# Seven products for 8 of 11 pairs of weight tiles instead of 5, made three and then four together, with weight sums made in DRAM

## The chip, the cores and the metric

One NeuronCore of a Trainium2 chip runs the whole program. The metric is the device time of one execution in microseconds, the median of several runs.

## The reference, cut to what matters

Two decoder layers on 512 positions of width 1024, all in float32. Each layer has a token mixer (multi-scale pooling in layer 0, differential attention in layer 1) and then the same gated feed-forward network, whose last product the change touches:

```python
def conv_ffn(h, w_up, conv_w, conv_b, w_down):      # h (1, 512, 1024), w_up (1024, 5632), w_down (2816, 1024)
    u = h @ w_up
    u = causal_dwconv(u, conv_w, conv_b)            # 3 taps along the positions
    a, g = jnp.split(u, 2, axis=-1)
    return (jax.nn.silu(g) * a) @ w_down

for i in range(DEPTH):
    ...
    x = x + conv_ffn(rmsnorm(x, norm_g[i, 1]), w_up[i], conv_w[i], conv_b[i], w_down[i])
return rmsnorm(x, final_norm)
```

## The kernel before, in words

**Precision.** A float32 product is three TensorE matmuls on rounded parts: each operand is split into `hi` (a cast on ScalarE, ACT) and `lo = x - hi` (a subtraction on VectorE, DVE), line 157 and 158, and `mm3` (lines 176 to 178) adds hi·hi, hi·lo and lo·hi in PSUM.

**The feed-forward network, `ffn`.** The up projection goes through 22 steps `f`. Each makes two tiles of 128 channels by 512 positions, 8 x 3 matmuls of 512 columns for the gate and as many for the value, and `gate` (convolution, silu, product) turns them into one activation tile. Weights come as chunks of 128 x 1024 (`chunk`): SyncE (SP) issues the load into one of 3 `raw` buffers, ACT and DVE split it into one each of 5 `hi` and 5 `lo` buffers.

**The down projection.** 22 activation tiles are 11 pairs `kk`. The output is x, four row tiles of 128 positions by two column halves `dh` of 512. For the last 6 pairs it is done the plain way (`pair`, weights from `pair_weights`): 2 column halves x 4 row tiles x 2 tiles x 3 matmuls. For the first 5 (`SEVEN`) a pair is a 2 x 2 block product, positions halved (`left`, `right`) and columns halved, done as in Strassen's method with seven block products. The activations' seven forms (differences of quarter blocks) are made by `forms` on DVE and split. The weights' forms are a block, a difference of two (on DVE, line 465) or a sum of two. A sum is made by DMA: SP loads one block into SBUF, and a GpSimd (POOL) DMA adds the other to it in place (line 461). `PLACES` says to which quarters of the output a product is added or subtracted (`put`, line 490); products 6 and 7 go to one quarter only and share PSUM banks with plain pairs. `GROUPS` packs the pairs' weights as two chunks for two pairs each and a half chunk for one.

**Order.** TensorE executes in the order of the program text. In the down projection that is the list of steps in `PASSES`, one string per column half: `p0` is plain pair 5, `5a` product 5 of the pairs of group a, `f2` the forms of pair 2, `e5` the additions of product 5, `k3` loads weights that are kept. The other engines' orders are fixed at compile time by a planner with its own costs, in which an instruction that comes earlier in the text goes first when both are ready. A buffer is taken from a pool when an earlier tile in it has been released. Forms of pairs 2 to 4 are made in the down projection (`LATE`), in the sixteen 512-column places of the two `H` buffers, which the up projection's input leaves free. The three plain pairs that are kept end the stage: per row tile 18 matmuls, the last addition, and `after`, which is the next stage's norm in layer 0 (`to_n2`) and the final norm and store in layer 1 (`finish`).

Of the kernel before, what the change touches and what calls it, by code (L numbers as in the profile page):

```python
# [38 lines left out]
SEVEN, LATE = 5, 2  # L39
GROUPS = (0, 2), (2, 2), (4, 1)  # L40


SIDES = {1: ((0, 0), ALU.subtract, (1, 1)), 2: ((0, 0), None, None), 3: ((0, 1), ALU.add, (1, 1)),
         4: ((1, 0), ALU.add, (0, 0)), 5: ((1, 1), None, None), 6: ((0, 0), ALU.add, (0, 1)),
         7: ((1, 0), ALU.add, (1, 1))}
PLACES = {1: ((0, 0, ALU.add), (1, 1, ALU.add)), 2: ((1, 0, ALU.add), (1, 1, ALU.subtract)),
          3: ((0, 1, ALU.add), (1, 1, ALU.add)), 4: ((0, 0, ALU.add), (1, 0, ALU.add)),
          5: ((0, 0, ALU.add), (0, 1, ALU.subtract)), 7: ((0, 0, ALU.add),)}

PASSES = ("p0 5a p1 f2 2a 7a f3 p2 f4 5b 5c e5 p3 2b 2c e2 p4 1a 1b p5 s 1c e1 7b 7c e7",  # L50
          "p0 4a 4b p1 4c e4 d 3a p2 3b 3c e3 6a 6b 6c k3 k4 k5")
# [26 lines left out]
def trunk(ctx, tc, x, norm_g, pool_w, pool_scale, kv_norm, w_kv, wq, lam, subln_g, wo,  # L78
# [10 lines left out]
    psum = ctx.enter_context(tc.tile_pool(name="psum", bufs=8, space=bass.MemoryType.PSUM))  # L89
    ctx.enter_context(tc.manual_schedule(engines={mybir.EngineType.PE}))  # L90
# [287 lines left out]
    def ffn(l, hT, cw, ws, pss, after):  # L378
# [13 lines left out]
        def gate(f, pg, pa):  # L392
            late = LATE <= f // 2 < SEVEN
# [12 lines left out]

        left, right = slice(0, HALF), slice(HALF, S)

        def forms(kk, room):


            a, b = act.pop(2 * kk), act.pop(2 * kk + 1)
            f = wide(f"f{l}_{kk}")
            less = ALU.subtract
            nc.vector.tensor_tensor(v3(f[:, :S], 2), v3(a, 2), b[:, right].unsqueeze(1).to_broadcast([P, 2, HALF]), less)
            nc.vector.tensor_tensor(f[:, S:S + HALF], a[:, left], b[:, left], less)
            nc.vector.tensor_tensor(f[:, S + HALF:], a[:, right], a[:, left], less)
            nc.vector.tensor_tensor(b[:, left], b[:, left], b[:, right], less)
            name = f"{l}_{kk}"
            both = room(f"fa{name}")  # L420
            split(a[:, left], both[:, left], both[:, right])
            form[kk, 3] = both[:, left], both[:, right]
            for src, one, two in (f[:, :S], 1, 2), (f[:, S:], 5, 6), (b, 7, 4):
                hi, lo = room(f"fh{name}_{one}"), room(f"fl{name}_{one}")
                split(src, hi, lo)
                form[kk, one] = cols((hi, lo), 0, HALF)
                form[kk, two] = cols((hi, lo), HALF, S)
# [17 lines left out]
        rooms = [v[:, i * S:(i + 1) * S] for v in halls for i in range(KD)]  # L445

        def room(name):
            return rooms.pop() if rooms else big(name)

        def block(kk, n, j, dh):  # L450

            src = w_down[l, kk * 2 * P:(kk + n) * 2 * P, dh * S:(dh + 1) * S]
            return src.rearrange("(k j p) c -> p j k c", j=2, p=P)[:, j]

        def product_weights(i, kk, n):
            name = f"d{l}_{i}_{kk}"
            first, op, other = SIDES[i]
            raw, hi, lo = chunk(block(kk, n, *first), n, S, name,
                                wide(f"rs_{name}")[:, :n * S] if op == ALU.add else None)
            if op == ALU.add:  # L460
                nc.gpsimd.dma_start(out=v3(raw, n), in_=block(kk, n, *other), accum_op=ALU.add)  # L461
            elif op:
                more = wide(f"raw2_{name}")[:, :n * S]
                nc.sync.dma_start(out=v3(more, n), in_=block(kk, n, *other))
                nc.vector.tensor_tensor(raw, raw, more, op)
            split(raw, hi, lo)
            return hi, lo

        def seven(i, kk, n, pss, first=None, last=None):

            w = product_weights(i, kk, n)
            for t in range(2):
                for k in range(n):
                    mm3(pss[t], cols(form[kk + k, i], t * P, (t + 1) * P), cols(w, k * S, (k + 1) * S),
                        kk + k == first, kk + k == last)
# [16 lines left out]
        def put_all(i):  # L492
            for half, dh, op in PLACES[i]:
                for t in range(2):
                    put(at[i][t], 2 * half + t, dh, op)

        at, kept = {}, []
        for dh in range(2):
            pss = [bank(f"pd{l}{dh}{t}") for t in range(NT)]
            at[7 - dh] = pss[2 * dh:2 * dh + 2]  # L500
            for step in PASSES[dh].split():
                if step[0] == "f":
                    forms(int(step[1:]), room)
                elif step[0] == "p":
                    kk = SEVEN + int(step[1:])
                    w = pair_weights(kk, dh)
                    for t in range(NT):
                        pair(pss[t], t, kk, w, kk == SEVEN, dh == 0 and kk == NF // 2 - 1 and t > 1)
                elif step[0] == "k":
                    kk = SEVEN + int(step[1:])  # L510
                    kept.append((kk, pair_weights(kk, dh)))
                elif step[0] == "e":
                    put_all(int(step[1:]))
                elif step[0] == "s":
                    for t in (2, 3):
                        put(pss[t], t, 0)
                elif step[0] == "d":
                    for t in range(NT):
                        after(t, 0)
                else:  # L520
                    i, (kk, n) = int(step[0]), GROUPS["abc".index(step[1])]
                    if i not in at:
                        at[i] = [bank(f"pd{l}_{i}{t}") for t in range(2)]
                    own = i < 6
                    seven(i, kk, n, at[i], 0 if own else None, SEVEN - 1 if own or i == 7 else None)
# [8 lines left out]
    def to_n2(t, dh):  # L534
        if dh == 0:
# [274 lines left out]
    def finish(t, dh):  # L810
        half_square(t, dh)
        if dh == 0:
# [55 lines left out]
```

## Time and profile before

| | us |
|---|---|
| median of 3 runs | 991.2 (990.95 to 993.31) |
| profiled execution, its own time | 991.5 |
| span of the profiled execution | 989.7 |
| PE busy | 978.0 (99%) |
| DVE busy | 641.8 (65%) |
| ACT busy | 451.0 (46%) |
| POOL busy | 113.5 (11%) |

Starting from 0, the up projection of layer 0 lies in about 40 to 280 us, its down projection to 394, attention to 640, and layer 1's up and down projections to the end. An operation is named out<-in with the program's names, buffer numbers left out: `pd<-hi_d,ah` is a matmul into a bank of the down projection from a weight chunk's high part and an activation's high part, `pu` one of the up projection, `raw_u` and `rs_d` weight buffers. Matmuls overlap, so the distance between their starts says more than the time of one.

### The profile page before, as it was taken

How to read it: one execution, taken by the hardware profiler on the slowest of the kernel's cores; microseconds unless marked ns; L12 is line 12 of the kernel's file. 1: busy time of each engine (PE TensorE's matmuls, PEld its weight loads, DVE VectorE, ACT ScalarE, POOL GpSimd, SP SyncE). 2: the span in 40 equal slices, each digit the busy share in tenths (PEclk: the TensorE clock that was granted, in tenths of full speed). 3: DMA queues.
4: the chain of work that ended last, by engine and by line, in shares of the span. 5: the costliest groups of instructions: out<-in, count | busy, mean ns of one | idle time of the engine just before them, and what ended most of it. 6: DMA issues, size and time to landing. Idle time of an engine off the chain costs nothing.

```text
span 989.7 us, 12569 instructions
## 1 busy us (share of the span) xinstructions
PE 978.0 (99%) x4810; PEld 826.9 (84%) x4810; DVE 641.8 (65%) x1000; ACT 451.0 (46%) x713; POOL 113.5 (11%) x137
## 2 busy tenths in 40 slices
PE   8999999999999999999999999999999999999997
PEld 8998888888888888788888887988888888888885
DVE  5877666665675545467867797687666656666553
ACT  5554334444462334346756763464334444452341
POOL 4500000000001111361220101000000000000211
PEclk9999999999999999999999999999999999999999
DMA  8333533323247963243213211233523233247952
GB/s 263 111 107 90 145 95 97 103 89 107 85 158 199 252 151 107 82 138 100 65 43 107 65 43 43 86 108 105 148 86 107 87 106 95 98 144 218 249 129 90
DMA packets 139783, 116.33 MB, mean 118 GB/s; under 512 B 4162, under 2 KB 112331, under 8 KB 139723
## 3 DMA queue, kind: packets, MB, share of 16 engines
q1 hardware_dynamic: 134218, 105.04, 34.0%
q0 software_dynamic: 5504, 10.49, 6.5%
q8 instruction: 38, 0.62, 0.3%
q14 instruction: 23, 0.18, 0.1%
HBM read 113.41 MB, written 2.10 MB: 117 GB/s over the span
## 4 chain that ended last, share of the span: by engine, by line
PE 96%; DVE 1%; DMA 1%; SPq 0%; issue 0%; POOL 0%; ACT 0%; DVEq 0%; POOLq 0%; ACTq 0%
PE pu L176 16%; PE pu L177 16%; PE pu L178 16%; PE pd L176 8%; PE pd L178 8%; PE pd L177 8%; PE sc L637 2%; PE po L666 2%; PE pw L178 2%; PE pj_k L178 1%; PE pj_k L176 1%; PE pj_k L177 1%; PE pj_q L177 1%; PE pj_q L176 1%; PE pj_q L178 1%; PE pw L177 1%
## 5 line engine op out<-in xcount | busy, mean ns | idle before, releaser
L158 DVE TENSOR_TENSOR lo_u<-raw_u,hi_u 128x1024 fp32r<-128x1024 f32 x84 | 103.2, 1231 | 122.7 <-ACT hi_u L157 122.5
L176 PE MATMUL pu<-n3h,hi_u 128*128 128x512 f32 (+1 forms) x384 | 142.9, 372 | 0.0
L176 PE MATMUL pu<-n1h,hi_u 128*128 128x512 f32 (+1 forms) x384 | 142.8, 372 | 0.0
L177 PE MATMUL pu<-n1l,hi_u 128*128 128x512 f32 (+1 forms) x384 | 142.6, 371 | 0.0
L177 PE MATMUL pu<-n3l,hi_u 128*128 128x512 f32 (+1 forms) x384 | 142.6, 371 | 0.0
L178 PE MATMUL pu<-n1h,lo_u 128*128 128x512 f32 (+1 forms) x384 | 142.6, 371 | 0.0
L178 PE MATMUL pu<-n3h,lo_u 128*128 128x512 f32 (+1 forms) x384 | 142.6, 371 | 0.0
L157 ACT CAST hi_u<-raw_u 128x1024 fp32r<-128x1024 f32 x84 | 88.3, 1053 | 106.9 <-PE pu L177 101.9
L461 POOL DMA_DIRECT2D rs_d<-in_w_down_dram x24 | 27.0, 1189 | 609.5 <-DMA rs_d<-in_w_down_dram 409.6
L176 PEld LDWEIGHTS pu<-n3h,hi_u 128*128 128x128 f32 x384 | 72.3, 188 | 12.6
L178 PEld LDWEIGHTS pu<-n3h,lo_u 128*128 128x128 f32 x384 | 72.3, 188 | 12.6
L177 PEld LDWEIGHTS pu<-n1l,hi_u 128*128 128x128 f32 x384 | 72.3, 188 | 12.5
L178 PEld LDWEIGHTS pu<-n1h,lo_u 128*128 128x128 f32 x384 | 72.3, 188 | 12.5
L176 PEld LDWEIGHTS pu<-n1h,hi_u 128*128 128x128 f32 x384 | 72.3, 188 | 12.4
L177 PEld LDWEIGHTS pu<-n3l,hi_u 128*128 128x128 f32 x384 | 72.3, 188 | 12.3
L176 PE MATMUL pd<-hi_d,ah 128*128 128x512 f32 x192 | 74.8, 389 | 0.0
L178 PE MATMUL pd<-hi_d,al 128*128 128x512 f32 x192 | 74.7, 389 | 0.0
L177 PE MATMUL pd<-lo_d,ah 128*128 128x512 f32 x192 | 74.7, 389 | 0.0
L157 ACT CAST hi_d<-raw_d 128x1024 fp32r<-128x1024 f32 (+1 forms) x42 | 41.7, 993 | 65.4 <-PE pd L178 48.1
L158 DVE TENSOR_TENSOR lo_d<-raw_d,hi_d 128x1024 fp32r<-128x1024 f32 (+1 forms) x42 | 47.5, 1147 | 32.7 <-ACT hi_d L157 32.7
L395 ACT ACTIVATE cv<-cv 128x512 f32<-128x512 f32 x44 | 27.8, 632 | 81.0 <-DVE cv L389 80.9
L387 ACT ACTIVATE cv<-pu,c_cb,c_cw 128x512 f32<-128x512 f32 x76 | 58.9, 776 | 0.0
(193 smaller groups left out, 1936.0 us busy)
## 6 DMA issues: line engine op xcount, KB each, us to landing
raw_u<-in_w_up_dram SPq DMA_DIRECT2D x88, 512.0 KB, 3.8
raw_d<-in_w_down_dram SPq DMA_DIRECT2D x40, 512.0 KB, 4.7
rs_d<-in_w_down_dram SPq DMA_DIRECT2D x16, 512.0 KB, 4.9
rs_d<-in_w_down_dram POOLq DMA_DIRECT2D x16, 512.0 KB, 7.1
raw_v<-in_w_kv_dram SPq DMA_DIRECT2D x8, 512.0 KB
raw_q<-in_wq_dram SPq DMA_DIRECT2D x8, 512.0 KB, 4.0
raw_k<-in_w_kv_dram SPq DMA_DIRECT2D x8, 512.0 KB
raw_o<-in_wo_dram SPq DMA_DIRECT2D x8, 512.0 KB, 3.4
```

What stands on the lines that cost most here:

```text
L157: nc.scalar.copy(hi, src)
L158: nc.vector.tensor_tensor(lo, src, hi, ALU.subtract)
L176: nc.tensor.matmul(ps, lh, rh, start=first, stop=False)
L177: nc.tensor.matmul(ps, lh, rl, start=False, stop=False)
L178: nc.tensor.matmul(ps, ll, rh, start=False, stop=last)
L387: nc.scalar.activation(y, ps, AF.Identity, bias=w[3], scale=w[2])
L395: nc.scalar.activation(y, y, AF.Silu)
L461: nc.gpsimd.dma_start(out=v3(raw, n), in_=block(kk, n, *other), accum_op=ALU.add)
L637: nc.tensor.matmul(ps[:, :m], qs[h, c][:, q], k[:, :m], start=not last, stop=bool(last))
L666: nc.tensor.matmul(po[h][:, qi * P:(qi + 1) * P], aT[:, kt * P:(kt + 1) * P], vt[kt][h // 4][:, (h % 4) * VD:(h % 4 + 1) * VD], start=kt = ...
```

## The change

Eight pairs, not five, go the way of seven products (`SEVEN` = 8), in four groups of two; three pairs stay plain. The list of steps is replaced by written loops with two passes. The first has products 5, 6 and 3 of each group in turn and then the plain pairs' right column half; the second has products 1, 4, 7 and 2 of each group in turn and then the plain pairs' left half, row tile by row tile. `forms` is cut into `forms_one` (products 5, 6, 3) and `forms_two` (1, 2, 7, 4). Forms of pairs 0 to 2 are made during the up projection, those of pairs 3 to 7 late, each call before the group or pair that it is written ahead of. A difference of weights is made on DVE from two loaded chunks. A sum of weights no longer goes through SBUF: during steps 2 to 17 of the up projection, one sum a step, POOL copies one block to a DRAM tile and adds the other to it there, paced by a small POOL instruction that reads the step's activation tile; the down projection then loads the sum as one chunk. In the diff `...` marks lines left out.

```diff
-SEVEN, LATE = 5, 2
-GROUPS = (0, 2), (2, 2), (4, 1)
...
+SEVEN, MADE = 8, 3
+SUMS = {6: ((0, 0), (0, 1)), 3: ((0, 1), (1, 1)), 7: ((1, 0), (1, 1)), 4: ((1, 0), (0, 0))}
...
             if f // 2 < SEVEN:
                 act[f] = a
                 if f % 2 and not late:
-                    forms(f // 2, big)
+                    forms_one(f // 2, [big(f"fa{l}_{f}{i}") for i in range(3)])
+                    forms_two(f // 2, [big(f"fb{l}_{f}{i}") for i in range(4)])
...
+            sum_weights(f, a)
...
+        def forms_one(kk, rooms):
+            a, b = act[2 * kk], act[2 * kk + 1]
+            f = scratch(f"f{l}_{kk}")
+            nc.vector.tensor_tensor(f[:, left], b[:, left], a[:, left], ALU.subtract)
+            nc.vector.tensor_tensor(f[:, right], a[:, right], a[:, left], ALU.subtract)
+            split(f, *rooms[:2])
+            split(a[:, left], rooms[2][:, left], rooms[2][:, right])
...
+        def forms_two(kk, rooms):
+            a, b = act.pop(2 * kk), act.pop(2 * kk + 1)
+            f = scratch(f"g{l}_{kk}")
+            nc.vector.tensor_tensor(v3(f, 2), v3(a, 2), b[:, right].unsqueeze(1).to_broadcast([P, 2, HALF]),
+                                    ALU.subtract)
+            nc.vector.tensor_tensor(b[:, left], b[:, left], b[:, right], ALU.subtract)
+            split(f, *rooms[:2])
+            split(b, *rooms[2:])
...
+        summed = {(g, i): dram.tile([P, 2 * S], F32, tag=f"sum{g}_{i}", bufs=2, name=f"sum{l}_{g}_{i}")
+                  for i in SUMS for g in range(SEVEN // 2)}
+        owing = list(summed)
+
+        def sum_weights(f, a):
+            if f < EARLY or not owing:
+                return
+            g, i = owing.pop(0)
+            pace = nc.gpsimd.tensor_scalar(small([P, 1], f"pace{l}_{f}"), a[:, :1], 1.0, None, ALU.add)
+            with tc.issue_after(pace.ins):
+                for blk, op in zip(SUMS[i], (ALU.bypass, ALU.add)):
+                    nc.gpsimd.dma_start(out=v3(summed[g, i], 2), in_=block(g, *blk), accum_op=op)
...
+        room = {kk: [halls.pop() for _ in range(3)] for kk in range(MADE, SEVEN)}
...
+        def of_sum(g, i, other=False):
+            return plain(v3(summed[g, i], 2), f"d{l}_{g}_{i}", other)[1]
+
+        def difference(g, one, name):
+            raw, hi, lo = chunk(block(g, 1, 1), 2, S, name, wide(f"rs_{name}"))
+            nc.vector.tensor_tensor(raw, one, raw, ALU.subtract)
+            split(raw, hi, lo)
+            return hi, lo
...
+        p5, c2, p3 = banks("5"), banks("6"), banks("3")
+        w0 = pair_weights(SEVEN, 1)
+        for t in (2, 3):
+            pair(c2[t - 2], t, SEVEN, w0, True)
+        for g in range(SEVEN // 2):
+            late_one(2 * g)
+            late_one(2 * g + 1)
+            seven(5, g, plain(block(g, 1, 1), f"d{l}_{g}_5")[1], p5)
+            seven(6, g, of_sum(g, 6), c2, False, False)
+            seven(3, g, of_sum(g, 3, True), p3)
+        put_all(5, p5)
+        put_all(3, p3)
+        c1 = banks("12")
+        for t in (0, 1):
+            pair(c1[t], t, SEVEN, w0, True)
+        for kk in range(SEVEN + 1, NP):
+            w = pair_weights(kk, 1)
+            late_two(MADE + kk - SEVEN - 1)
+            for t in range(NT):
+                pair((c1 + c2)[t], t, kk, w, last=kk == NP - 1)
+        for t in range(NT):
+            put((c1 + c2)[t], t, 1)
...
+        p1, p4 = banks("1"), banks("4")
+        c1, p2 = banks("7"), banks("2")
+        for g in range(SEVEN // 2):
+            for kk in (2 * g, 2 * g + 1):
+                if kk >= MADE + NP - SEVEN - 1:
+                    late_two(kk)
+            raw, w2 = plain(block(g, 0, 0), f"d{l}_{g}_2")
+            w1 = difference(g, raw, f"d{l}_{g}_1")
+            end = g == SEVEN // 2 - 1
+            if end:
+                seven(2, g, w2, p2)
+            seven(1, g, w1, p1)
+            seven(4, g, of_sum(g, 4), p4)
+            seven(7, g, of_sum(g, 7, True), c1, True, False)
+            if not end:
+                seven(2, g, w2, p2)
+        put_all(2, p2)
+        put_all(1, p1, (0,))
+        put_all(4, p4, (0,))
+        kept = [(kk, pair_weights(kk, 0)) for kk in range(SEVEN, NP)]
+        c2 = banks("21")
         for t in range(NT):
             for kk, w in kept:
-                pair(pss[t], t, kk, w, last=kk == NF // 2 - 1)
-            put(pss[t], t, 1)
-            after(t, 1)
+                pair((c1 + c2)[t], t, kk, w, t > 1 and kk == SEVEN, kk == NP - 1)
+            put((c1 + c2)[t], t, 0)
+            after(t, 0, True)
+            if t == 0:
+                put_all(1, p1, (1,))
+                put_all(4, p4, (1,))
+                for i in (2, 3):
+                    after(i, 1, False)
```

## Rows read from the trace of the kernel before

**Rows 1.** Page, engine totals: busy us, share of the span, instructions.

```profile
PE 978.0 (99%) x4810; PEld 826.9 (84%) x4810; DVE 641.8 (65%) x1000; ACT 451.0 (46%) x713; POOL 113.5 (11%) x137
```

**Rows 2.** By stretch: us, PE, PEld, DVE, ACT, POOL busy, clock, DMA share, GB/s.

```profile
60.00:279.90 219.90, 219.90 (x981) 182.48 (x980) 143.75 (x184) 95.08 (x124) 1.40 (x1) 1.00 0.36 105
279.90:391.00 111.10, 111.10 (x496) 92.06 (x495) 65.08 (x90) 41.91 (x55) 15.66 (x16) 1.00 0.69 185
640.00:871.00 231.00, 231.00 (x1068) 193.24 (x1067) 149.70 (x195) 101.30 (x131) 1.28 (x1) 1.00 0.35 102
...
320.00:340.00 20.00, 20.00 (x90) 16.53 (x90) 13.15 (x18) 6.42 (x8) 4.52 (x4) 1.00 0.96 239
868.50:880.00 11.50, 11.50 (x52) 9.51 (x52) 9.64 (x16) 9.91 (x18) 0.00 (x0) 1.00 0.35 115
```

**Rows 3.** PE's waits: who for whom, us in total, times, longest.

```profile
PE dps L324 <- DVE h L214: 1.3, 1, 1.3
PE pv L178 <- DVE n2l L158: 0.7, 1, 0.7
```

**Rows 4.** Timeline of PE, down projection of layer 0: start, us, line, operands.

```profile
279.69 0.39 PE L178 MATMUL pu<-n1h,lo_u 128*128 128x512 f32 x1
279.92 0.39 PE L176 MATMUL pd<-hi_d,ah 128*128 128x512 f32 x1
...
388.49 0.39 PE L178 MATMUL pd<-hi_d,al 128*128 128x512 f32 x1
```

**Rows 5.** Tile pd on PE: ns min/median/max, first and last start, form.

```profile
L176 PE MATMUL pd<-hi_d,ah x192: 389/389/477, 279.9 to 981.9; 128*128 128x512 f32 x192
```

**Rows 6.** DVE groups by shape: count, busy us, mean ns, idle before.

```profile
L158 DVE TENSOR_TENSOR lo_d<-raw_d,hi_d 128x1024 fp32r<-128x1024 f32 x36 | 43.5, 1223 | 30.9 <-ACT hi_d L157 30.9
L490 DVE TENSOR_TENSOR x<-x,pd 128x512 f32<-128x512 f32 x56 | 35.6, 683 | 14.1 <-PE pd L178 13.8
L158 DVE TENSOR_TENSOR fl<-f,fh 128x512 fp32r<-128x512 f32 x10 | 6.9, 685 | 0.0
L465 DVE TENSOR_TENSOR raw_d<-raw_d,raw_d 128x1024 f32<-128x1024 f32 x4 | 4.9, 1225 | 11.0 <-DMA raw_d<-in_w_down_dram 11.0
L417 DVE TENSOR_TENSOR f<-ar 128x256 f32<-128x256 f32 x6 | 2.6, 425 | 0.2
```

**Rows 7.** ACT groups by shape, columns as in rows 6.

```profile
L157 ACT CAST hi_d<-raw_d 128x1024 fp32r<-128x1024 f32 x36 | 38.0, 1054 | 47.9 <-PE pd L178 32.6 <-DVE raw_d L465 10.0 <-PE pu L177 5.0
L157 ACT CAST hall<-f 128x512 fp32r<-128x512 f32 x10 | 5.8, 616 | 0.0
L157 ACT CAST hall<-ar 128x256 fp32r<-128x256 f32 x6 | 2.4, 403 | 1.9 <-PE pu L177 1.9
```

**Rows 8.** POOL; queues at 300:360, 125:265; landings of rs_d, raw_u; ACT's wait, 60:279.9.

```profile
L461 POOL DMA_DIRECT2D rs_d<-in_w_down_dram x24 | 27.0, 1189 | 609.5 <-DMA rs_d<-in_w_down_dram 409.6
...
L196 POOL TENSOR_SCALAR r_n<-ssq_n 128x1 f32<-128x1 f32 x16 | 6.8, 423 | 63.5 <-ACT sq_n L206 63.4
...
rs_d<-in_w_down_dram POOLq DMA_DIRECT2D x16, 512.0 KB, 7.1
...
q1 hardware_dynamic: 5068, 9.69, 47.7%
q0 software_dynamic: 2064, 3.93, 39.7%
...
q1 hardware_dynamic: 23968, 13.63, 32.5%
...
114.22 1.40 POOL L461 DMA_DIRECT2D rs_d<-in_w_down_dram  x1 [70.64 <-DVE cv L388]
...
DMA to landing us min/median/max: 3.6/3.8/4.9
...
ACT hi_u L157 <- PE pu L177: 44.1, 33, 3.7
```

**Rows 9.** Timeline of the end: start, us, engine, line, operation.

```profile
982.77 0.69 DVE L490 TENSOR_TENSOR x<-x,pd 128x512 f32<-128x512 f32 x1
```

More of the change, by code (lines that the diff above doesn't have):

```diff
@@ L89, in trunk @@
     psum = ctx.enter_context(tc.tile_pool(name="psum", bufs=8, space=bass.MemoryType.PSUM))
+    dram = ctx.enter_context(tc.tile_pool(name="dram", bufs=1, space=bass.MemoryType.DRAM))
     ctx.enter_context(tc.manual_schedule(engines={mybir.EngineType.PE}))
@@ L392, in gate @@
         def gate(f, pg, pa):
-            late = LATE <= f // 2 < SEVEN
+            late = MADE <= f // 2 < SEVEN
             y = conv(pg, NF + f, f"{l}_{NF + f}")
@@ L405, in gate @@
                 act[f] = ah, al
+            sum_weights(f, a)
         left, right = slice(0, HALF), slice(HALF, S)
-        def forms(kk, room):
-            a, b = act.pop(2 * kk), act.pop(2 * kk + 1)
[L413 to L427, printed above, removed]
+        def forms_one(kk, rooms):
[5 more added lines that the diff above has]
+            split(a[:, left], rooms[2][:, left], rooms[2][:, right])
+            form[kk, 5], form[kk, 6] = cols(rooms[:2], 0, HALF), cols(rooms[:2], HALF, S)
+            form[kk, 3] = rooms[2][:, left], rooms[2][:, right]
@@ new lines, in forms_two @@
+        def forms_two(kk, rooms):
+            a, b = act.pop(2 * kk), act.pop(2 * kk + 1)
+            f = scratch(f"g{l}_{kk}")
[4 more added lines that the diff above has]
+            split(b, *rooms[2:])
+            form[kk, 1], form[kk, 2] = cols(rooms[:2], 0, HALF), cols(rooms[:2], HALF, S)
+            form[kk, 7], form[kk, 4] = cols(rooms[2:], 0, HALF), cols(rooms[2:], HALF, S)
@@ L444, in ffn @@
         halls = [hp.tile([P, KD * S], F32R, tag="H", bufs=2, name=f"hall{l}{i}") for i in range(2)]
[L445 to L465, printed above, removed]
+        halls = [v[:, i * S:(i + 1) * S] for v in halls for i in range(KD)]
@@ new lines, in ffn, with late_one, late_two, plain @@
+        room = {kk: [halls.pop() for _ in range(3)] for kk in range(MADE, SEVEN)}
+        def late_one(kk):
+            if kk >= MADE:
+                forms_one(kk, room[kk])
+        def late_two(kk):
+            if kk >= MADE:
+                forms_two(kk, room[kk] + [big(f"fb{l}_{kk}")])
+        def plain(src, name, other=False):
+            raw, hi, lo = chunk(src, 2, S, name, wide(f"rs_{name}") if other else None)
+            split(raw, hi, lo)
+            return raw, (hi, lo)
+        def of_sum(g, i, other=False):
+            return plain(v3(summed[g, i], 2), f"d{l}_{g}_{i}", other)[1]
@@ L466, in product_weights, with seven @@
+        def difference(g, one, name):
+            raw, hi, lo = chunk(block(g, 1, 1), 2, S, name, wide(f"rs_{name}"))
+            nc.vector.tensor_tensor(raw, one, raw, ALU.subtract)
             split(raw, hi, lo)
             return hi, lo
-        def seven(i, kk, n, pss, first=None, last=None):
-            w = product_weights(i, kk, n)
+        def seven(i, g, w, pss, first=True, last=True):
             for t in range(2):
-                for k in range(n):
-                    mm3(pss[t], cols(form[kk + k, i], t * P, (t + 1) * P), cols(w, k * S, (k + 1) * S),
-                        kk + k == first, kk + k == last)
+                for k in range(2):
+                    kk = 2 * g + k
+                    mm3(pss[t], cols(form[kk, i], t * P, (t + 1) * P), cols(w, k * S, (k + 1) * S),
+                        first and kk == 0, last and kk == SEVEN - 1)
@@ L490, in put, with put_all @@
             nc.vector.tensor_tensor(part, part, ps, op)
-        def put_all(i):
+        def put_all(i, pss, halves=(0, 1)):
             for half, dh, op in PLACES[i]:
                 for t in range(2):
[L495 to L525, printed above, removed]
@@ new lines, in put_all, with banks @@
+                    if half in halves:
+                        put(pss[t], 2 * half + t, dh, op)
+        NP = NF // 2
+        def banks(name):
+            return [bank(f"pd{l}_{name}{t}") for t in range(2)]
+        p5, c2, p3 = banks("5"), banks("6"), banks("3")
[8 more added lines that the diff above has]
+            seven(3, g, of_sum(g, 3, True), p3)
@@ new lines, in ffn @@
+        put_all(5, p5)
[10 more added lines that the diff above has]
+            put((c1 + c2)[t], t, 1)
+        for t in (0, 1):
+            after(t, 1, False)
+        p1, p4 = banks("1"), banks("4")
@@ L532, in trunk, with to_n2 @@
     n2 = Normed("n2", None)
-    def to_n2(t, dh):
-        if dh == 0:
+    def to_n2(t, dh, last):
+        if not last:
             return
@@ L808, in half_square, with finish @@
                              accum_out=fssq[:, 2 * t + dh:2 * t + dh + 1])
-    def finish(t, dh):
+    def finish(t, dh, last):
         half_square(t, dh)
-        if dh == 0:
+        if not last:
             return
```

14 lines of the change are left out of this document (6 added, 8 removed).

## The prediction

> **What bounds the kernel now.** I read the engine totals first: TensorE (PE) is busy 978 of 989.7 us, VectorE (DVE) 642, ScalarE (ACT) 451 [rows 1]. A busy total alone doesn't prove a bound, so the second view is the table by stage. In the up projections of both layers and in the down projection of layer 0, PE is busy for the whole of every stretch (219.9 of 219.9 us, 111.1 of 111.1, 231.0 of 231.0) at a granted clock of 1.00; DVE is busy for 59% of the down stage of layer 0 (65.08 us) and ACT for 38% [rows 2]. Third come PE's waits: the longest is 1.3 us, near the start, and the one nearest to a stage that changes is 0.7 us, just after layer 0's down stage [rows 3]. Fourth, the pace. The last `pu` matmul starts at 279.69, the first `pd` at 279.92, and the 480th `pd` of layer 0, the last ahead of the final row tile's 18, at 388.49 [rows 4]: (388.49 - 279.92) / 479 = 0.2267 us from start to start. The 389 ns of one matmul [rows 5] overlap with the next and are not the price; 0.2267 us is. So the down stages cost their number of matmuls times 0.2267 us, as long as nothing else runs late. What remains is to count matmuls and then to ask what may run late.
>
> **The change part by part.**
>
> *Matmuls removed.* A pair of weight tiles takes 2 column halves x 4 row tiles x 2 x 3 = 48 matmuls the plain way (6 pairs x 48 x 2 layers = 576, three rows of 192 [rows 5]) and 7 products x 2 x 3 = 42 by seven products. Before: 6 x 48 + 5 x 42 = 498 a layer. After: 3 x 48 + 8 x 42 = 480. All are 512 columns wide in both versions. 18 fewer a layer, 36 in all: 36 x 0.2267 = **8.16 us** less PE, all on the path, since PE has no idle time there.
>
> *DVE in the down stage.* Weight splits: 26 full and 7 half remainders a layer become 34 full: 34 x 1.223 - 26 x 1.223 - 7 x 0.69 = +5.0 us. Differences of weights: two full and one half become four full, at 1.225 us, +1.8. Forms made late: three pairs become five. One costs 0.69 + 3 x 0.42 for the differences, 3 x 0.69 + 0.42 for the remainders, 4.45 us, whether in one call or two: +8.9. The additions to x stay 28 of 0.68 us a layer [rows 6]. So 65.1 + 15.7 = 80.8 us [rows 2] in a stage of 111.1 - 4.1 = 107.0: 76%. ACT: +4.1 for splits and two more late forms of 3 x 0.62 + 0.40 = 2.25 us, +4.5 [rows 7]: 50.5 us, 47%. By totals both hide behind PE; if that cover fails, each microsecond late is one of time.
>
> *The tightest stretches.* In the first pass a group of two pairs is three chunks of 12 matmuls, 36 x 0.2267 = 8.2 us of PE; DVE owes 3 x 1.22, and in groups 2 and 3 two calls of `forms_one` (0.42 + 0.42 + 0.69 + 0.42 = 1.95) besides: 7.6 of 8.2. In the second pass a group is four chunks, 10.9 us; DVE owes 4 x 1.22 + 1.22, and in the last group two calls of `forms_two` (2.49 each): 11.1 of 10.9, in the one before 8.6, in the first two 6.1. The slack is the run-ahead: with five hi/lo buffers (four in the first pass, where `w0` holds one throughout) a split can start three or four chunks, 8.2 or 10.9 us, before its products, and needs 1.05 + 1.22 = 2.3 of that. If DVE idled for a whole cast (1.05) at every chunk, it would fall behind by 2 x 2.6 = 5.1 us in the first pass against 5.9 of spare, and by 1.9 + 4.4 = 6.3 in the second against 8.6. So it takes more than one such idle cast a chunk, about 1.2, to reach PE. I count **0**, and keep 0 to 4 us a layer as bounds.
>
> *Work that moves into the up projections.* One more pair's forms (4.45 us of DVE, 2.25 of ACT) a layer: DVE is at 143.75 of 219.9 there [rows 2], hidden.
>
> *Sums in DRAM.* Gone from the down stage: 12 accumulations a layer, in which DMA stood at 0.96 of its engines for 20 us without PE noticing [rows 2]. New, in steps 2 to 17 of the up projection: 16 sums, each a POOL instruction (0.42 us), a copy DRAM to DRAM and an accumulation, every one with an issue of 1.19 us on POOL [rows 8]. The accumulation waits on POOL for the copy to land; queued behind it are only the next step's pair, since POOL does nothing else there (1.4 us of 219.9 [rows 2]). With a landing like the 7.1 us of today's accumulation a step of POOL is 0.42 + 1.19 + 7.1 + 1.19 = 9.9 us, within the 10.9 us (48 matmuls) that a step gives; a lag could grow through the four steps that are left, 43 us. Price on the DMA engines: in 300 to 360 us q0 spends 39.7% x 60 x 16 / 2064 = 185 ns on a 2 KB packet, q1 90 ns; 256 packets make 512 KB, so an accumulation is 3.0 us of all 16 engines and a plain load 1.4. The `w_up` loads take 0.325 of the engines at 30 ns a packet [rows 8]. No row has DRAM as the target of a sum; from below I take 1.4 + 3.0 us a sum, from above both as twice the accumulation, 12.0. A step then needs 3.6 + 4.4 = 8.0 to 15.6 us of DMA out of 10.9. I take the lower, nearest to the rows: **0** on PE. Even 15.6 would not reach PE at once: with 3 raw and 5 hi/lo buffers a load is issued seven chunks (38 us) ahead and lands in 3.8 us, 4.9 at most [rows 8]. There is no gain in it either, since PE has no wait there to lose.
>
> *A rule against it.* That maximum of 4.9 us covers a stretch with one accumulation beside `w_up` loads (the one POOL issues at about 114 us). The Trainium skill ("DMA: Bandwidth & Descriptors", Queues, rings and completion order) says that each DMA engine serves its queue rows in turn, a packet at a time. By that rule, with q0 never empty, a `w_up` chunk would wait a long sum packet for each of its short ones and take 64 x (30 + 185) ns = 13.8 us, over the 5.44 that PE gives it; by the row it stays under 5. The row can't settle sums that follow one another closely; this is the last rival below.
>
> *Loads of the down stage.* 38 plain loads a layer, 38 x 1.44 = 55 us of DMA in 107, less than today's 0.69 [rows 2]; the densest stretch, five loads in 10.9 us, is 7.2 us. Zero.
>
> *Seams.* PSUM: the first pass starts with six banks and takes the other two; the second needs banks that the additions free one matmul group earlier. At layer 0's end four more additions (2.7 us of DVE) fall between the rows of x that become `n2`, where PE already waits 0.7 us for DVE [rows 3]. PE runs 18 matmuls (4.1 us) per row tile there, so I allow **0.3 us**. Layer 1 still ends in one addition, square, scale and store, 982.77 to 989.7 [rows 9]: unchanged.
>
> Sum against the profiled execution: 991.5 - 8.16 + 0.3 = 983.6 us (its span of 989.7 plus 1.8 around it). The median of the runs is 991.2, 0.3 below that execution; so **983.3 us**.
>
> **The rivals.**
>
> *Partial gain.* DVE's or ACT's order leaves some chunk late, 1 to 2.3 us a layer at the two tight stretches (11.1 of 10.9 in the last group of the second pass). For: DVE goes from 59 to 76% of the stage, and it takes its instructions in a fixed order. Against: no such wait today at up to 9.64 of 11.5 us of DVE around layer 1's seam [rows 2]. Time: 985.4 to 988.
>
> *Slower, by DVE.* If DVE idles two casts (2.1 us) at each chunk, the first pass is late by 2 x 5.7 - 5.9 = 5.5 us and the second by 2 x 3.6 + 6.1 + 8.6 - 8.6 = 13.3 us; 18.8 a layer, 38 in all: 983.3 + 38 = 1021. It decides from 4.1 us of waiting a layer, about 1.4 casts a chunk. Against: today's waits of ACT for PE before its casts are slack of just this kind (in the up stage of layer 0, 44.1 us [rows 8]), and a late chunk would use them up first. The same mechanism at the point where it just eats the gain gives 988 to 994.
>
> *Slower, by DMA.* If sums in DRAM cost four times today's accumulation (12 us + 1.4), a layer needs 16 x 13.4 + 20 x 3.6 = 286 us of DMA in 20 x 10.9 = 218; less the 38 us of lead, PE stands 30 us a layer: 983.3 + 60 = 1043. It decides from about 10.4 us an accumulation, 3.5 times the row. For: no row has DRAM as the target of a sum, and 0.325 of the engines is already taken. Against: the landings of 3.6 to 4.9 us beside one accumulation [rows 8]. (The Trainium skill's rule above speaks for it, and for starved loads from a lower price on.)
>
> **How the numbers follow.** A measurement of this kernel can't tell less than 0.3%, 3 us, from no change. Forecast as counted, 982 to 985: 0.62. Partial gain, 985 to 988.2: 0.16. Gain eaten, 988.2 to 994.2: 0.09. Slower by DVE 0.07, by DMA 0.06. Faster 0.78, same 0.09, slower 0.13. The matmuls alone give 991.2 - 8.2 = 983.0, and runs of one kernel lie up to 2 us apart, so the low end is 981.5; the high end takes in the partial gain, 989.
>
> **What would show it.** Right: 480 `pd` matmuls a layer, still 0.227 us apart; both down stages 4.1 us shorter; `raw_u` landings under some 10 us with DMA at 0.7 to 0.9 in the up stages; no row of `pd` waiting for DVE or ACT. Wrong: PE waiting for `lo_d` or a form in the last groups of a pass (DVE); PE waiting for `hi_u` or `lo_u` in the up stages, POOL's sums running past step 21 (DMA); `pv` waiting over 1 us at layer 0's end (seam).

## The result and the profile after

Four runs of each kernel: 985.75 us after (984.66 to 986.76), 991.59 before (990.95 to 993.31). The ratio is 0.9938, 95% interval 0.9921 to 0.9955. The profiled execution of the changed kernel took 985.66 us, its span 983.9. The engine totals, to be held against [rows 1]:

```profile
PE 971.1 (99%) x4774; PEld 822.2 (84%) x4774; DVE 667.5 (68%) x1040; ACT 464.3 (47%) x727; POOL 152.9 (16%) x209
```

The table by stage, columns as in [rows 2]: up projection and down projection of layer 0, the 20 us in which DMA stood at 0.96 before, then the up and down projections of layer 1.

```profile
60.00:280.50 220.50, 220.50 (x986) 183.06 (x986) 138.71 (x177) 93.83 (x123) 33.26 (x48) 1.00 0.71 186
280.50:391.00 110.50, 110.50 (x498) 91.66 (x496) 85.19 (x123) 53.85 (x71) 4.25 (x7) 1.00 0.41 137
320.00:340.00 20.00, 20.00 (x90) 16.57 (x89) 15.77 (x24) 7.26 (x8) 0.00 (x0) 1.00 0.56 188
642.00:867.50 225.50, 225.50 (x1029) 188.16 (x1028) 142.88 (x181) 97.58 (x126) 33.23 (x48) 1.00 0.71 184
867.50:976.30 108.80, 108.80 (x482) 90.10 (x480) 81.60 (x109) 47.47 (x66) 2.58 (x6) 1.00 0.37 126
```

PE is still busy for the whole of all four long stretches, at a granted clock of 1.00, and makes 36 matmuls less (x4774 against x4810). The first 462 `pd` of each layer start 0.2267 us apart, as before. DVE has taken on 20 us in layer 0's down stage, and DMA has moved from the down stages (0.69 to 0.41) to the up stages (0.36 to 0.71). The five waits of PE that the view lists, columns as in [rows 3] (`sc` are the scores of attention, `dps` belongs to the start, `pw` to the product at attention's end, `pv` is the first product of attention):

```profile
PE sc L689 <- DVE kl L672: 1.6, 1, 1.6
PE dps L319 <- DVE h L209: 1.4, 1, 1.4
PE warm L139 <- DVE ones L134: 1.0, 1, 1.0
PE pw L171 <- ACT oh L157: 0.8, 1, 0.8
PE pv L173 <- DVE n2l L153: 0.7, 1, 0.7
```

None belongs to a stage that the change touches, and the first, in the attention of layer 1, is new. Splitting both spans at the first matmul of each stage gives the account of the 5.8 us between them:

| stretch | before, us | after, us | difference |
|---|---|---|---|
| start to the first up matmul | 36.8 | 37.3 | +0.5 |
| up projection, layer 0 | 243.1 | 243.1 | 0 |
| first `pd` to first `pv` | 114.6 | 110.5 | -4.1 |
| attention | 232.2 | 233.8 | +1.6 |
| up projection, layer 1 | 243.0 | 243.0 | 0 |
| down projection, layer 1 | 112.7 | 108.6 | -4.1 |
| last `pd` to the end | 7.4 | 7.6 | +0.2 |

So each down stage gave 4.08 us, together the 8.16 that 36 matmuls cost, and 2.3 us went elsewhere. What these 2.3 us are is the first question for the experiments; the second is how near the change came to its rivals (sums in DRAM, DVE), which no wait of this trace shows.

### The profile page after: what moved, and what is told of

It reads as the page before. It is cut to its first block, busy times and chain, and to the rows that moved or that the text cites. A ratio compares the mean times of both kernels' runs of the same rounds, so it can differ in the third digit from the quotient of the medians.

```text
span 983.9 us, 12623 instructions
## 1 busy us (share of the span) xinstructions
PE 971.1 (99%) x4774; PEld 822.2 (84%) x4774; DVE 667.5 (68%) x1040; ACT 464.3 (47%) x727; POOL 152.9 (16%) x209
## 3 DMA queue, kind: packets, MB, share of 16 engines
q0 software_dynamic: 13312, 33.56, 15.6%
## 4 chain that ended last, share of the span: by engine, by line
PE 94%; DVE 2%; DMA 1%; POOL 1%; ACT 1%; issue 1%; SPq 0%; DVEq 0%; POOLq 0%; ACTq 0%
PE pu L171 16%; PE pu L173 16%; PE pu L172 16%; PE pd L173 7%; PE pd L172 7%; PE pd L171 7%; PE sc L689 2%; PE po L718 2%; PE pw L173 2%; PE pj_k L171 1%; PE pj_k L172 1%; PE pj_k L173 1%; PE pw L172 1%; PE pw L171 1%; PE pj_q L171 1%; PE pj_q L172 1%
## 5 line engine op out<-in xcount | busy, mean ns | idle before, releaser
L153 DVE TENSOR_TENSOR lo_u<-raw_u,hi_u 128x1024 fp32r<-128x1024 f32 x84 | 103.2, 1231 | 144.2 <-ACT hi_u L152 144.0
L447 POOL DMA_DIRECT2D sum<-in_w_down_dram x64 | 58.5, 913 | 150.6 <-DMA sum<-in_w_down_dram 141.9
L153 DVE TENSOR_TENSOR lo_d<-raw_d,hi_d 128x1024 fp32r<-128x1024 f32 x44 | 53.6, 1222 | 27.3 <-ACT hi_d L152 27.2
L152 ACT CAST hi_d<-raw_d 128x1024 fp32r<-128x1024 f32 x44 | 46.4, 1054 | 52.0 <-PE pd L173 36.3
L171 PE MATMUL pd<-hi_d,hall 128*128 128x512 f32 x140 | 54.5, 389 | 0.0
L172 PE MATMUL pd<-lo_d,hall 128*128 128x512 f32 x140 | 54.5, 389 | 0.0
L382 ACT ACTIVATE cv<-pu,c_cb,c_cw 128x512 f32<-128x512 f32 x68 | 52.6, 774 | 0.3
L384 DVE SCALAR_TENSOR_TENSOR cv<-pu,c_cw,cv 128x510 f32<-128x510 f32 x68 | 50.9, 748 | 2.1
```

What stands on the lines that cost most here:

```text
L152: nc.scalar.copy(hi, src)
L153: nc.vector.tensor_tensor(lo, src, hi, ALU.subtract)
L171: nc.tensor.matmul(ps, lh, rh, start=first, stop=False)
L172: nc.tensor.matmul(ps, lh, rl, start=False, stop=False)
L382: nc.scalar.activation(y, ps, AF.Identity, bias=w[3], scale=w[2])
L384: nc.vector.scalar_tensor_tensor(y[:, 2:], ps[:, :S - 2], w[0], y[:, 2:], ALU.mult, ALU.add)
```

## The experiments

**Is the 1.6 us of attention part of the change?** The program text of attention, and the order of its instructions on each engine, are the same in both kernels. The timeline around the new wait shows DVE's `lo_q` taking 2.82 us beside a POOL multiplication of `raw_q` by the norm's gain (start, duration, engine, operation, idle before):

```profile
438.31 1.90 POOL L641 TENSOR_TENSOR raw_q<-raw_q,c_gn 128x1024 f32<-128x1024 f32 x1 [1.42 <-DMA raw_q<-in_wq_dram]
438.48 2.82 DVE L153 TENSOR_TENSOR lo_q<-raw_q,hi_q 128x1024 fp32r<-128x1024 f32 x1 [1.86 <-ACT hi_q L152]
...
441.32 0.68 DVE L672 TENSOR_TENSOR kl<-pj_k,kh 64x512 fp32r<-64x512 f32 x1
...
442.15 0.36 PE L689 MATMUL sc<-kl,qs 128*128 128x256 f32 x1 [1.55 <-DVE kl L672]
...
442.35 0.40 PE L171 MATMUL pj_q<-n2h,hi_q 128*128 128x512 f32 x1
...
442.58 0.40 PE L172 MATMUL pj_q<-n2l,hi_q 128*128 128x512 f32 x1
```

So: the changed kernel again, unaltered, and before with 18 matmuls a layer left out by another edit (`e2`), so that its result lacks their products:

```diff
-                    for t in range(NT):
+                    for t in range(1 if (dh, kk) == (0, 7) else NT):
                         pair(pss[t], t, kk, w, ...)
```

> The changed kernel unaltered, for a second profile and a tighter ratio. Both down projections were 4.1 us shorter in the first profile; 0.55 us was lost at the start (clock 0.66 in 10 to 20 us), 1.55 us at the first scores in attention, 0.2 at the end. Theory A (attention's wait is a fixed collision in time between a GpSimd multiply and a VectorE subtraction, the start is chance): the wait of 1.5 us at the scores is there again, the start may differ by 0.5 us either way; time 985 to 986.5. Rival B (both are chance): the wait is gone or elsewhere, and executions scatter between 983 and 987.

> The kernel before with 18 matmuls of the down projection left out in each layer (row tiles 1 to 3 of the third plain pair, first column half), all else as it was: no sums in DRAM, no new order. Theory A (36 fewer matmuls are worth 8.16 us where they stand, whatever the rest): both down projections 4.1 us shorter, time 983.4 plus what attention's timing happens to cost, 0 to 1.6 us. Rival C (the changed kernel's new work costs 2.3 us somewhere): this kernel gives the full 8.2 us, 983.4, with no new wait.

`e1_again`: 984.27 us (983.73 to 984.65), ratio 0.9914 (0.9899 to 0.9929). Its profile has no wait at `sc`. Here DVE came first, by 0.05 us:

```profile
438.64 1.23 DVE L153 TENSOR_TENSOR lo_q<-raw_q,hi_q 128x1024 fp32r<-128x1024 f32 x1 [1.71 <-ACT hi_q L152]
438.69 2.94 POOL L641 TENSOR_TENSOR raw_q<-raw_q,c_gn 128x1024 f32<-128x1024 f32 x1 [1.48 <-DMA raw_q<-in_wq_dram]
...
439.90 0.68 DVE L672 TENSOR_TENSOR kl<-pj_k,kh 64x512 fp32r<-64x512 f32 x1
```

Whichever of the two starts first runs at its own length (1.90 or 1.23 us), the other ends some 3 us after its start. `e2` took 987.07 us (983.49 to 989.69) where 983.4 was expected, so wide that its median tells nothing about the 1.6 us; its mean granted clocks go with it, 0.998 in the run of 983.49 and 0.991 in that of 989.69. Its profiled execution is the one of 983.49, 8.0 under the 991.5 of before, and its row of layer 0's down stage is:

```profile
279.60:390.10 110.50, 110.50 (x498) 91.69 (x496) 67.48 (x94) 44.93 (x62) 16.46 (x18) 1.00 0.69 186
```

Eighteen matmuls less give 110.5 us here too, with the forms, sums and DMA of before. So the gain of the down stage is that of the number of matmuls; the new order and the sums in DRAM neither add to it nor take from it there.

Next the multiplication was taken out of `project`, in the changed kernel (`e3`) and in before (`e4`), whose results then lack the gains:

```diff
-        nc.gpsimd.tensor_tensor(v3(raw, KD), v3(raw, KD), spread(g, P), ALU.mult)
```

> The changed kernel without the GpSimd multiplication of the query and key weights by their norm gains (16 instructions; the gains are left out of the result). Theory A: no GpSimd operation lies beside VectorE's subtraction, the wait of 1.5 us at the first scores goes, time 1.5 us or a little more under the changed kernel, about 984.2. Rival B: the scores wait all the same for kl, no change.

> The kernel before without the same 16 GpSimd multiplications. Theory A: it had no wait at the scores, so nothing to gain, 991.2 to 991.6; the difference to e3 is then 7.4 to 8.2 us. Rival C: it gains as much as e3 does and the difference stays 5.8 us.

`e3`: 983.48 us (982.53 to 985.67), 0.9909 (0.9894 to 0.9924); `lo_q` takes 1.22 us, PE doesn't wait at `sc`, and attention is 231.2 us long, 2.6 less than in the profile after. `e4`: 991.42 us, 0.9985 (0.9977 to 0.9994), attention 231.2 us against 232.2. With the collision out of both kernels their medians are 7.9 us apart (7.4 to 8.2 expected), near the 8.16 of the matmuls. A third set of runs of the changed kernel shows the collision again, POOL ahead by 0.02 us:

> The changed kernel unaltered, third profile. Theory B' (its first 2.3 us under the forecast's gain were chance: start, one collision in attention): 983.5 to 985, both down projections 4.1 us shorter, attention without a wait at the scores or with the same 1.5 us, in which case the scatter over executions is made of it.

```profile
438.11 1.90 POOL L641 TENSOR_TENSOR raw_q<-raw_q,c_gn 128x1024 f32<-128x1024 f32 x1 [1.55 <-DMA raw_q<-in_wq_dram]
438.13 2.95 DVE L153 TENSOR_TENSOR lo_q<-raw_q,hi_q 128x1024 fp32r<-128x1024 f32 x1 [1.86 <-ACT hi_q L152]
```

986.05 us (983.09 to 987.26), 0.9927 (0.9909 to 0.9944), above the 985 that was expected at most. Of the twelve kept profiles with the multiplication, three have POOL first (after, `e1_third` and `e9` below, by 0.17, 0.02 and 0.15 us), and these three have the wait, of 1.6 to 1.7 us. In the other nine DVE is first, by 0.05 to 0.76 us, and none has it. So the order of the two starts decides. In the three profiles of before and its variants DVE leads by 0.23 to 0.76 us, in the unaltered changed kernel by 0.05 us or not at all; whether the change makes the collision more frequent was not settled by so few.

**How near was DMA?** `e5` makes every sum twice, the second into DRAM tiles that nobody reads:

```diff
+        again = {(g, i): dram.tile([P, 2 * S], F32, tag=f"again{g}_{i}", bufs=2, name=f"again{l}_{g}_{i}")
+                 for g, i in summed}
...
                 for blk, op in zip(SUMS[i], (ALU.bypass, ALU.add)):
+                    for to in summed, again:
-                    nc.gpsimd.dma_start(out=v3(summed[g, i], 2), in_=block(g, *blk), accum_op=op)
+                        nc.gpsimd.dma_start(out=v3(to[g, i], 2), in_=block(g, *blk), accum_op=op)
```

> The changed kernel with every DRAM sum made twice (a second set of DRAM tiles, never read). In the changed kernel q0 took 43.7% and q1 37.2% of the DMA engines in 80 to 250 us, 184 ns a q0 packet. Theory D (w_up loads and sums share the engines, and starve PE once both no longer fit): a step needs 3.9 + 11.8 = 15.7 us of DMA out of 10.9, 16 steps overrun by 77 us less the four free steps (28) and the 38 us of lead, so PE loses some 11 us a layer: about 1006, with PE waiting for hi_u or lo_u. Rival E (the sums alone fall behind, loads keep their share): raw_u lands in under 10 us, POOL's issues run past step 17, time 984 to 985.

1105.1 us (1103.19 to 1120.62), ratio 1.1182 (1.1114 to 1.1251), where 1006 or 984 was expected: the cliff is there, less than twice the sums away, but it is not the one that I had described. The up projections took 267.4 and 266.7 us instead of 243, the down stages 146.1 and 144.0 instead of 110.5 and 108.6, so 71 of the 119 us were lost in the down stages. PE stood for 90 of the 119; the rest went while it was busy, at mean granted clocks of 0.97 in the up and 0.88 in the down stages. The table by stage for 36 us in which PE did not stand, for two stalls of PE in the up projection and for the longest in the down stage:

```profile
126.00:162.00 36.00, 36.00 (x160) 29.80 (x160) 10.08 (x13) 6.45 (x8) 7.60 (x10) 1.00 0.63 136
166.80:172.90 6.10, 0.00 (x0) 0.00 (x0) 0.01 (x1) 1.08 (x2) 0.68 (x1) 0.77 0.94 256
200.40:207.20 6.80, 0.00 (x1) 0.00 (x0) 0.00 (x0) 1.03 (x2) 0.69 (x2) 0.78 1.07 296
308.10:324.60 16.50, 0.01 (x1) 0.01 (x1) 2.91 (x5) 2.40 (x4) 3.81 (x5) 0.56 0.58 120
```

In these stalls of the up projection the DMA engines were full (0.94 and 1.07), but before them they had room (0.63), and in the down stage they had it while PE stood (0.58). The waits say what stood behind what (waiter, whom for, us in total, times, longest; they are links of the same chains and not to be added up), and SP's timeline shows the queue itself:

```profile
SPq L166 <- DMA sum<-in_w_down_dram: 169.7, 8, 36.1
ACT hi_u L152 <- DMA raw_u<-in_w_up_dram: 126.7, 15, 30.7
ACT cv L382 <- POOL pace L446: 81.5, 4, 33.1
PE pd L171 <- ACT hi_d L152: 48.4, 4, 16.6
PE pu L171 <- ACT hi_u L152: 31.6, 7, 7.7
```

```profile
117.41 8.37 SPq L166 DMA_DIRECT2D raw_u<-in_w_up_dram  x3
161.88 0.35 SPq L166 DMA_DIRECT2D rs_d<-sum  x1
```

SP issues in a fixed order, and the planner put the loads of four sums (`rs_d<-sum`, product 3, whose buffers are free early) among the `raw_u` loads. From 126 to 162 us SP issued nothing, as the sum was not made; the `raw_u` loads behind it were late, and ACT and PE waited for them.

A second path is the pace instruction: it reads the activation tile, lags with POOL, and holds the buffer that the next convolution needs. It is what the longest stall of the down stage goes back to, for ACT has the cast of the weights (`hi_d`) behind that convolution (POOL and ACT, PE's stall ends at 324.60):

```profile
319.12 0.72 POOL L446 TENSOR_SCALAR pace<-cv 128x1 f32<-128x1 f32 x1
319.88 0.78 ACT L382 ACTIVATE cv<-pu,c_cb,c_cw 128x512 f32<-128x512 f32 x1 [33.02 <-POOL pace L446]
323.50 1.04 ACT L152 CAST hi_d<-raw_d 128x1024 fp32r<-128x1024 f32 x1
```

Both paths start at POOL. Its 16 pace instructions of layer 0 run from 78.87 to 336.12 us, 17.1 us from one to the next, while a step of PE takes 11: each round of two copies and two accumulations begins when the one before is issued, and the last sum is issued at 343.71, 39 us into the down stage. What POOL waits for between its issues the profile mostly doesn't show ("issue", 355 us ahead of `again`). In the unaltered kernel a copy, the wait for it and an accumulation take 7 us of a step (pace at 219.79, accumulation issued by 226.7), and POOL then waits for the next activation tile.

The in-order wait of SP is in the unaltered changed kernel too, hidden by the lead of `raw_u` (its SP waits and timeline):

```profile
SPq L166 <- DMA sum<-in_w_down_dram: 73.5, 8, 10.1
```

```profile
103.25 22.13 SPq L166 DMA_DIRECT2D raw_u<-in_w_up_dram  x5
135.46 0.35 SPq L166 DMA_DIRECT2D rs_d<-sum  x1
```

**Were sums in DRAM needed at all?** `e6` keeps eight pairs but makes the sums in SBUF during the down projection, as before did, without `sum_weights`:

```diff
-            sum_weights(f, a)
...
         def of_sum(g, i, other=False):
-            return plain(v3(summed[g, i], 2), f"d{l}_{g}_{i}", other)[1]
+            name = f"d{l}_{g}_{i}"
+            raw, hi, lo = chunk(block(g, *SUMS[i][0]), 2, S, name, wide(f"rs_{name}") if other else None)
+            nc.gpsimd.dma_start(out=v3(raw, 2), in_=block(g, *SUMS[i][1]), accum_op=ALU.add)
+            split(raw, hi, lo)
+            return hi, lo
```

> The changed kernel with the sums made as before: one block loaded into SBUF in the down projection, the other added there by a POOL DMA; the order, the eight pairs and the rest stay. Theory F (the eight pairs fit only with the sums taken out of the down projection): a second-pass group needs 5 loads x 1.4 + 2 x 3.0 = 13.2 us of DMA in 10.9, a first-pass group 10.3 in 8.2; both passes run out of their lead, PE waits some 2 to 10 us a layer for hi_d: 988 to 1004. Rival G (the SBUF sums would have been hidden as they were): 984 to 985.

1015.94 us (1014.84 to 1016.47), ratio 1.0231 (1.0213 to 1.0249): slower than before, though it has the 480 matmuls of the changed kernel. Layer 0's down stage is 121 us instead of 110.5, layer 1's 122 instead of 108.6. Of the 16 sums of layer 0 ten are made in that stage, from 292 to 370 us, 5.7 to 15.2 us apart, and three of these ten start after a wait for a load to land. Three in a row on POOL's timeline:

```profile
300.75 1.22 POOL L470 DMA_DIRECT2D rs_d<-in_w_down_dram  x1 [7.22 <-DMA rs_d<-in_w_down_dram]
306.49 1.21 POOL L470 DMA_DIRECT2D raw_d<-in_w_down_dram  x1 [4.52 <-DVE g L420]
321.64 1.22 POOL L470 DMA_DIRECT2D rs_d<-in_w_down_dram  x1 [13.93 <-DMA rs_d<-in_w_down_dram]
```

A sum takes some 17 us on this way: from 323.54 to 340.33 us the chain that ended last has a load (5.8 us), an accumulation (7.8), a cast (1.05) and a subtraction (1.24) one after another, and then the next load. The DMA engines were at 0.64 of the stage. After a wait of PE its matmuls come 0.43 us apart for a while, twice the 0.2267 of [rows 4], while the granted clock of the slice from 316 to 320 us is 0.67:

```profile
313.77 0.51 PE L171 MATMUL pd<-hi_d,hall 128*128 128x512 f32 x1 [1.13 <-ACT hi_d L152]
315.03 0.61 PE L172 MATMUL pd<-lo_d,hall 128*128 128x512 f32 x1 [0.75 <-DVE lo_d L153]
315.44 0.63 PE L173 MATMUL pd<-hi_d,hall 128*128 128x512 f32 x1
...
318.00 0.63 PE L173 MATMUL pd<-hi_d,hall 128*128 128x512 f32 x1
318.43 0.51 PE L171 MATMUL pd<-hi_d,hall 128*128 128x512 f32 x1
```

```profile
316.00:320.00 4.00, 4.00 (x14) 3.18 (x13) 4.00 (x7) 3.96 (x7) 0.00 (x0) 0.67 0.83 253
```

The direction was as expected; the price was not (988 to 1004). PE stood for 5.7 and 8.2 us in the two stages, within the 2 to 10 a layer that had been expected. Some 10 us more of the stages went while PE was busy, at mean clocks of 0.99 and 0.97, and 7 us at the start and in attention. That PE's waits come from the chain of loads and accumulations rather than from full DMA engines is read from the trace; no run separates the two.

**How near was DVE?** `e7` and `e9` add useless work to DVE ahead of the split of 24 of the 34 weight chunks a layer (the sums and two of the plain blocks of each group), 512 columns in `e7` and 1024 in `e9`:

```diff
+    zero = const.tile([P, 1], F32, name="zero")
+    nc.gpsimd.memset(zero, 0.0)
...
+            nc.vector.tensor_tensor(raw[:, :512], raw[:, :512], zero[:, :1].to_broadcast([P, 512]), ALU.add)
             split(raw, hi, lo)
```

> The changed kernel with one more VectorE operation on the path of 28 of the 34 weight chunks a layer (adds zero to 512 columns of the loaded chunk, about 0.69 us each, 19 us a layer). VectorE was busy 85.2 us of the 111.1 that hold layer 0's down projection. Theory H (what counts is VectorE's total: PE waits only once it passes the stage's 107 us): 85 + 19 = 104, PE waits 0 to 3 us a layer: 984 to 990. Rival I (VectorE's fixed order already leaves bubbles that a chunk's extra step turns into waits): 5 us a layer or more, 994 and up.

> The changed kernel with a VectorE operation of 1024 columns (about 1.22 us) on the path of 24 of the 34 weight chunks a layer, 29 us a layer. (e7 put one of 512 columns there, on 24 chunks and not 28 as its expectation said: 16.4 us a layer, and lost nothing, with VectorE at 92.8 of 109.3 us.) Theory H (VectorE's total counts): 85 + 29 = 114 us against 107, PE waits 3 to 8 us a layer for lo_d or hi_d: 990 to 1000. Rival L (still hidden, because part of it lies in the up projection's time and VectorE's operations overlap at their ends): 984 to 986.

`e7`: 984.16 us (983.09 to 984.51), 0.9910 (0.9893 to 0.9927). `e9`: 984.69 us (983.61 to 985.31), 0.9914 (0.9893 to 0.9935), with these down stages:

```profile
279.80:390.30 110.50, 110.50 (x498) 91.66 (x496) 101.58 (x140) 54.22 (x71) 4.25 (x7) 1.00 0.44 141
867.10:975.90 108.80, 108.80 (x482) 90.08 (x480) 98.16 (x127) 48.12 (x67) 2.59 (x6) 1.00 0.40 130
```

DVE is at 92% and 90% of the stage, and PE does not wait there. The expectation had counted all 24 additions into the stage, 114 us of DVE, and had PE waiting; nine of the 24 ran before the stage, ahead of the chunks that are loaded early, so the stage holds 15 of them and DVE never passed PE's time (rival L). What happens beyond it was not tried. For the kernel as it is, DVE's rival is refuted with 16 us to spare in the stage, and with it the partial gain, which was to come from the same place.

**The start.** In the profile after, PE ran at a granted clock of 0.66 from 10 to 20 us, and at 0.50 (the lower level, 1.2 GHz) from 13 to some 19; shortly before, up to 10.1 us, it had waited 1.4 us for DVE:

```profile
10.00:20.00 10.00, 9.86 (x58) 9.86 (x59) 9.42 (x16) 5.06 (x10) 4.04 (x4) 0.66 1.07 370
13.00:19.00 6.00, 6.00 (x30) 6.00 (x30) 6.00 (x10) 4.06 (x8) 4.04 (x4) 0.50 1.07 382
```

In before the same slice is at 1.00, with the same instructions. `e8` and `e10` put six more small matmuls ahead of that wait, in the changed kernel and in before; `e8_again` repeats `e8`:

```diff
-... h1 i0 s0 m0 i1 ...
+... h1 i0 W6 s0 m0 i1 ...
```

> The changed kernel with six more warm-up matmuls of 128 columns (about 0.22 us each) between the pooling matmuls of row tiles 0 and 1, where PE stood idle for 1.4 to 1.7 us. In two profiles of the changed kernel the granted clock fell to 0.50 between 13 and 19.5 us, 3 to 4 us after that idle time, and up projections began 0.55 and 1.1 us later. Theory J (the idle time lets the clock fall, in some executions only): no stretch at 0.50, mean clock 0.998 or 0.999 in every execution, times 983.3 to 984.3 with less scatter. Rival K (the clock falls by chance whatever PE did just before): means of 0.993 to 0.996 still occur.

> The kernel before with the same six warm-up matmuls. Theory A: the distance between this and the changed kernel with them is the matmuls' 8.16 us, 7.5 to 8.8 measured, since the start is then alike in both: 991.0 to 991.6 here.

> The changed kernel with six more warm-up matmuls, again, beside the changed kernel itself on the same chip. Theory J: 0.5 to 1 us faster than the changed kernel in the median, no stretch at clock 0.50 in the first 30 us. Rival K: no difference that shows.

`e8`: 983.27 us (982.91 to 985.37), 0.9909 (0.9892 to 0.9926). `e8_again`: 984.45 us (982.82 to 985.71), 0.9915 (0.9898 to 0.9931). `e10`: 991.66 us (990.94 to 992.92), 0.9992 (0.9982 to 1.0002). Both profiles of `e8` have 1.00 in that slice, but so have `e9` and `e1_third` without the extra matmuls and with the same wait, of 1.4 and 2.0 us. The profile of `e10`, which has the extra matmuls and not this wait, has 0.83. Its dip follows another wait, of 0.9 us up to 15.9. So the wait at 10 us is neither enough for a dip nor needed for one. The intervals overlap with those of the unaltered kernel, and `e10` lies 7.2 us over `e8_again`, where 7.5 to 8.8 was expected. That the dip comes and goes from one execution to another is shown, and that it goes with the first up matmul at 37.3 us or later (37.3 to 37.9 in after, `e1_again`, `e5`, `e7` and `e10`, 39.4 in `e6`) instead of 36.4 to 37.0; that more warm-up prevents it, or that `e8` is the faster version, is not.

## Why the prediction was right, point by point

**Matmuls removed: right.** 8.16 us forecast, 8.16 measured in the two down stages. Every profile of a kernel with 480 `pd` matmuls a layer and undisturbed loads has 110.5 us in layer 0 and 108.6 in layer 1; before, `e4` and `e10`, with 498, have 114.6 and 112.7.

**DVE in the down stage: right in sign, 4 us short, of no effect.** 80.8 us were forecast for layer 0; 85.2 were used (81.6 in layer 1). Two of the four are in the base: its 65.1 us cover 111.1 of the 114.6 us of the stage before, and the whole stage had 67.1. "The tightest stretches" counted 0 for PE, and `e9` shows that the run-ahead covers more than that: 16 us more DVE in the stage cost nothing.

**Sums in DRAM: the price was near, the mechanism of danger was not the one I named.** Over the whole program the queue of the sums took

```profile
q0 software_dynamic: 13312, 33.56, 15.6%
```

15.6% x 983.9 us / 32 sums = 4.8 us of all 16 engines a sum (a copy and an accumulation), against 4.4 taken and 12 as the upper bound. A `raw_u` load of layer 0's up stage landed in 4.8 us at the median and 6.0 at most, where I had said under 10 (before 3.8 and 4.9 [rows 8]). The thirteen-microsecond load of the rule that I weighed did not appear, not even in `e5` (6.8 and 9.0), where POOL issued one transfer after another. POOL's last sum of layer 0, the one paced by step 17, was issued at 247.06 us, before the up projection ended at 280, as planned. What I left out is that a load of a sum, too, is an instruction in SP's queue, ahead of other loads: 73.5 us of waiting in the unaltered kernel, all of it hidden. In `e5` the engines' time alone would have fitted: 27.6% x 1101.4 us / 64 sums = 4.75 us a sum, 9.5 for two, so by the rival's own account 16 x 9.5 + 20 x 3.6 = 224 us of DMA in 218 and 38 of lead. What decided was POOL's step, which the prediction had at 9.9 of 10.9 us, which took 7 in the unaltered kernel and grew to 17.1 here, and what waits for POOL: SP's queue and the buffer that the pace instruction holds. The sign "POOL's sums running past step 21" was right; the rival "Slower by DMA" had a nearer threshold than its 10.4 us an accumulation, by a path that I had not seen.

**Loads and seams.** DMA in the down stages fell to 0.41 and 0.37. The prediction counted 38 loads a layer; there are 34, which changes nothing. `pv` waits 0.7 us as before, so the 0.3 us allowed for the seam was not needed.

**What was missing from the sum: 2 us, by one execution.** The profiled execution is 2.1 us over the 983.6 of the sum: +1.6 in attention, +0.5 at the start, +0.2 at the end, less the 0.3 of the seam. No term stood for these, as nothing of the change runs there. The runs show that neither belongs to every execution: `e1_again` has attention at 231.8 us and is 1.4 us shorter, `e1_third` has no dip of the clock. Over 14 executions of the unaltered changed kernel the median is 985.0 us (983.09 to 987.26), 1.7 over the forecast. The collision in attention explains part. Long executions tend to have a lower mean granted clock (987.26 us at 0.992, 983.09 at 0.998), but not all do (986.76 at 0.998, 984.38 at 0.994), and why the times differ stays open. Held against the executions of before taken beside them, the three sets of the unaltered changed kernel are 5.8, 7.7 and 6.1 us faster, all below the 7.9 forecast. So 985.75 missed the band "as counted", 982 to 985, and lies in that of the rival "Partial gain", but not by its mechanism, since no row of `pd` waits: that the stated range reached so far, on that rival's account, was luck.

## What to carry to other kernels

Where PE is busy for the whole of a stage, count matmuls times the distance between their starts, and expect just that. Before moving work to an idle resource, write down for each new instruction which in-order queue it stands in, whom it waits for, and what stands behind it: here sums made twice cost 12% over the changed kernel, because loads and a buffer stood behind POOL's series of transfers. And repeat the profile before explaining a microsecond in a stage that wasn't touched: two engines that start 0.02 us apart may change places.

## What the runs showed of the hardware

A DVE subtraction of 128 x 1024 takes 1.22 us alone and 2.82 to 2.95 beside a POOL multiplication that started first; POOL's takes 1.90 alone and 2.94 when DVE was first. The second ends about as long after the first as its own length, so they ran one after the other. The Trainium skill ("SBUF — State Buffer", SBUF: two separate sides) says that these two engines share a pair of ports under an exclusive lock which is held for a whole instruction, so that the other is blocked (on VectorE's side also by an operation with two inputs in SBUF, as this subtraction has); the three pairs above agree with it, and show that 0.02 us in the order can cost TensorE 1.7 us.

Unexpected too was what a short stall of PE leaves behind. In `e6` waits of 1.13 and 0.75 us were followed by nine matmuls that start from 315.03 to 318.43 us, eight distances in 3.40 us instead of the 1.81 that they take at 0.2267: 1.6 us more, nearly as much as the two waits themselves. The granted clock of that slice, 0.67, lies between the two levels (0.50 is 1.2 GHz, 1.00 is 2.4 GHz), and the matmuls stand at the distance of the lower one. The 1.55 us wait at `sc` in the profile after has no such tail: the matmuls behind it start at 442.35 and 442.58, 0.23 us apart. What tells the two cases apart was not tried.
